# Down projection from 2x2 block products, and a swap of two pools in attention, in a one-core decoder layer

## The chip, the core and the metric

The kernel runs on one core of a Trainium2 chip. The core has five engines with a queue of instructions each: TensorE (PE) multiplies matrices, VectorE (DVE), ScalarE (ACT) and GpSimd (POOL) work on elements, SyncE (SP) mostly issues DMA transfers, which ACT and POOL can issue too. Each engine takes its instructions in the order of its queue, and an instruction whose inputs are not there holds up everything behind it. The metric is the device time of one execution in microseconds (us), lower is better. Three runs of the kernel before gave 1781.09, 1783.0 and 1796.59 us, the median is 1783.0 us.

## The reference

One decoder layer, for a prompt of 1024 tokens and 8 sample tokens (1032 columns in all), in fp32, with D_MODEL = 1024 and D_FF = 2816:

```python
x = x + jnp.concatenate([o_attn, o_gdn], axis=-1) @ w_out   # top-k attention and a gated delta rule
x = x + mem_attend(rmsnorm(x, xattn_norm_g), mem_k, mem_v, w_mq, mq_norm_g, w_mo)
hf = rmsnorm(x, ffn_norm_g)
x = x + (jax.nn.silu(hf @ w_gate) * (hf @ w_up)) @ w_down
```

The change is in the last line's `@ w_down` (2816 rows, 1024 columns) and, by the place of two pools in memory, at the start of `o_attn`.

## The kernel before

Activations lie transposed: features on the 128 partitions, tokens along the free axis. Every fp32 operand is split into a rounded high part and a rest (`wh`, `wl` for weights, `AH`, `AL` for activations, `kh`, `kl` for keys), and every product is three matmuls, high by high, high by rest, rest by high. `split_w` (L125, L126) makes the parts of a weight block with a cast on ACT (`wh`) and a subtraction on POOL (`wl`), each with two buffers; `split` (L143, L144) makes those of an activation with a cast on ACT and a subtraction on DVE.

**Attention.** After the projections, the keys are stacked in `kh` and `kl` (`stack_k`, L490 to L493: ACT casts, POOL copies, a DVE subtraction, in pieces of 256 tokens). The normed queries `qn` are stored to a DRAM scratch `qscr0` to `qscr2` by ACT's queue (L476), and loaded back in blocks of 128 tokens as `qld` by SP's queue (L500) and split into `qst` (L502 to L505, ACT and DVE). The first product of queries and keys is `plg` on PE. `kh` and `kl` lie in the pool `pp`, `qld` and `qst` in `uA`. A pool lies on the left or the right stack of SBUF, and its tiles wait for the last use of whatever lay in the same place: `k1`, the scratch of the top-k searches, was on the right.

**Feed-forward.** The 2816 hidden features are done in 11 units of 256. The gate and up products of a unit already come from 2x2 block products (`unit_product`): sums of weight blocks on DVE (`S`, L1851), their parts on ACT and POOL (`sh`, `sl`, L1856, L1857), and for gate and for up five products of 24 matmuls of 260 columns on PE into `p`, which DVE adds up (`uu`, `s`, L1881); then SiLU on ACT, and three products of gate and up on POOL (L1915), which SP's queue stores to the scratch `scrF`, 22 tiles of 128 features by 1032 tokens. The fourth quarter of each unit (`sg`) is made and stored before the units begin (`early`).

**Down projection.** `stage_down` fetches the tiles back (`fetch`: `af`, then `AH` and `AL` or `dh` and `dl`), in three passes over features 0 to 7, 8 to 14 and 15 to 21. For each of the 8 output blocks of 128 features, `down` loads a weight block (L115, 512 or 448 KB) and multiplies for the token groups of 512, 256 and 264 columns into `pd`: 22 x 8 x 3 x 3 = 1584 matmuls. DVE adds each `pd` into `xT` (L1928), which was loaded with the residual from `scrT` (L1963, L1968). In the last pass `store_y` transposes each finished output block on PE (`py`, L51) and stores it.

The order on each queue is set by a scheduler ahead of time, from its own model of durations and from the order in the program; at run time the queues are fixed.

Of the kernel before, what the change touches and what calls it, by code (L numbers as in the profile page):

```python
# [6 lines left out]
F32 = mybir.dt.float32  # L7
FR = mybir.dt.float32r
BF = mybir.dt.bfloat16
I32 = mybir.dt.int32  # L10
# [3 lines left out]
OP = mybir.AluOpType  # L14
# [25 lines left out]
class Kernel:  # L40
# [111 lines left out]

    def consts(self):
        nc, c = self.nc, self.c
        jp = c.tile([128, 128], I32, name="jp")
# [1660 lines left out]
    def first(self, u, kind, s1, p, sg):  # L1816

        V = self.nc.vector
        if kind == "gate":
            V.tensor_add(sg[:, 0], s1, p)  # L1820
            self.silu(sg[:, 0], sg[:, 0])
        else:
            V.tensor_add(sg[:, 1], s1, p)  # L1823
            self.nc.gpsimd.tensor_mul(sg[:, 1], sg[:, 0], sg[:, 1])
            self.nc.sync.dma_start(self.scrF[2 * u, :, 0:HN], sg[:, 1])

    def unit_product(self, u):

        nc, V = self.nc, self.nc.vector
# [7 lines left out]
        for kind in ("gate", "up"):  # L1837
# [31 lines left out]
            def product(j, op, name):  # L1869
                h, l = parts[j]  # L1870
                banks = []
                for c in halves:
                    p = self.bank("g", name)
                    for k in range(4):
                        self.three(p[:, :w // 2], h[:, k], l[:, k], *ops[op](k, c), k == 0, k == 3)
                    banks.append(p)
                return banks

            def plus(out, x, banks):
                for p, c in zip(banks, halves):  # L1880
                    V.tensor_add(out[:, c], x[:, c], p[:, :w // 2])  # L1881

            if kind == "gate":
# [16 lines left out]
                self.first(u, kind, s1[:, :HN], p, sg[0])  # L1900
            p5 = product(1, "T1", "p5")
            plus(u2, u1, product(3, "T3", "p7"))
            plus(u1, u1, p5)
# [3 lines left out]
            c = [u1, u2[:, :HN], s1]  # L1907
            if kind == "gate":
                for x in c:
                    self.silu(x, x)  # L1910
                sg["c"] = c
            else:
                f = 2 * u
                for x, y, dst in zip(c, sg["c"], (self.scrF[f, :, HN:], self.scrF[f + 1, :, 0:HN], self.scrF[f + 1, :, HN:])):
                    nc.gpsimd.tensor_mul(x, x, y)  # L1915
                    nc.sync.dma_start(dst, x)

    def down(self, f0, acts, groups, last=False):
        nc, V = self.nc, self.nc.vector
        kt = len(acts)  # L1920
        for o in range(KD):
            wh, wl = self.load_w(self.i["w_down"][0][128 * f0:128 * (f0 + kt), 128 * o:128 * o + 128], kt, 128)
            for g in groups:
                g0, n = self.G[g]
                p = self.bank("g", "pd")
                self.proj(wh, wl, 0, 128, g, p, kt=kt, act=lambda k: [x[:, g0:g0 + n] for x in acts[k]])
                x = self.xT[:, o, g0:g0 + n]
                V.tensor_add(x, x, p[:, :n])  # L1928
            if last:
                self.store_y(o)  # L1930

    def store_y(self, o):
        nc = self.nc
        cs = slice(128 * o, 128 * o + 128)
        for half in range(2):
            p = self.bank("g", "py")
            for t in range(4):
                c = 128 * (4 * half + t)
                self.tr(p[:, 128 * t:128 * t + 128], self.xT[:, o, c:c + 128], 128)
            y = self.unit("y", [128, 4, 128])  # L1940
            (nc.vector.tensor_copy if half else nc.scalar.copy)(y, p.rearrange("p (t c) -> p t c", c=128))
            nc.sync.dma_start(self.o["y_prompt"][0, 512 * half:512 * half + 512, cs].rearrange("(t p) c -> p t c", p=128), y)
        p = self.bank("g", "py")
        self.tr(p[:NS, :128], self.xT[:, o, T:NT], 128)
        y = self.unit("y8", [NS, 128])
        nc.scalar.copy(y, p[:NS, :128])
        nc.scalar.dma_start(self.o["y_sample"].rearrange("b o d -> (b o) d")[:, cs], y)

    def fetch(self, f, h, l, s):

        a = self.unit("af")[:, :s.stop - s.start]
        self.nc.sync.dma_start(a, self.scrF[f, :, s])
        self.split(a, h[:, s], l[:, s])

    def stage_down(self, after_units):

        acts = [(self.AH[:, k], self.AL[:, k]) for k in range(KD)]
        n1, n2, n = slice(0, HN), slice(HN, NT), slice(0, NT)
        for f in range(8):
            self.fetch(f, *acts[f], n1)  # L1960
        after_units()
        for o in range(KD):
            self.nc.sync.dma_start(self.xT[:, o, n1], self.scrT[:, o, n1])  # L1963
        for f in range(8):
            self.fetch(f, *acts[f], n2)
        self.down(0, acts, (0,))
        for o in range(KD):
            self.nc.sync.dma_start(self.xT[:, o, n2], self.scrT[:, o, n2])  # L1968
        self.down(0, acts, (1, 2))
        more = [[self.du.tile([128, UW], FR, name="d" + x, tag="d")[:, :NT] for x in "hl"] for _ in range(7)]  # L1970
        for f in range(8, 15):
            self.fetch(f, *more[f - 8], n)
        self.down(8, more, (0, 1, 2))
        for f in range(15, 22):
            self.fetch(f, *acts[f - 15], n)
        self.down(15, acts[:7], (0, 1, 2), True)


    def build(self):
# [7 lines left out]
        self.AH = self.act.tile([128, KD, NT], FR, name="AH")  # L1987
        self.AL = self.act.tile([128, KD, NT], FR, name="AL")
# [30 lines left out]
        for p in (self.sm, self.gp, self.tk, self.hp, self.fp, self.lop, self.wp, self.k1, self.ps):  # L2019
# [18 lines left out]
        for p in (self.pp, self.sm, self.gp, self.late, self.lg, self.up, self.scp, self.keep, self.ps):  # L2038
# [5 lines left out]
        self.scrT, self.scrF = self.dr.tile([128, KD, NT], F32, name="scrT"), self.dr.tile([22, 128, NT], F32, name="scrF")  # L2044
# [16 lines left out]
        self.ps = P(name="psG", bufs=1, space=PSUM)  # L2061
        self.gv = P(name="gv", bufs=1)
        self.gw = P(name="gw", bufs=1)
        for u in range(11):
            self.unit_product(u)

        def after_units():
            for p in (self.tp, self.gw, self.gv):
                p.release()
            self.keep = P(name="keepD", bufs=1)  # L2070
            self.xT = self.keep.tile([128, KD, NT], F32, name="xT")
            self.du = P(name="du", bufs=14)

        self.stage_down(after_units)
        for p in (self.wp, self.du, self.keep, self.u, self.act, self.c, self.dr, self.ps):
            p.release()

    def sample_gen(self):
# [33 lines left out]
```

## Time and profile before

| | |
|---|---|
| runs | 1781.09, 1783.0, 1796.59 us |
| the profiled execution | 1778.02 us, its span 1776.0 us, mean granted PE clock 0.952 |
| busy share | PE 92%, DVE 61%, ACT 50%, POOL 46% |
| the units | from about 1177 to 1500 us |
| the down projection | from about 1500 to 1771 us |

A row of a window gives the busy time of each engine in it and, behind it in brackets, the number of instructions; "PEclk" is the granted clock as a share of full speed, "GB/s" what the DMA engines moved. In a row of the chain of waits stand the start, the time that the piece took and what it was; the chain goes back from the end of the run, so a piece that is not PE is one for which PE stood. A row of an operation gives its name by line, its count, and its shortest, median and longest duration in ns.

### The profile page before, as it was taken

To read this page: it belongs to the slowest core of one execution; us is meant where nothing else is said; L and a number is where in the kernel's file an instruction comes from. 1 tells how busy PE (TensorE), PEld (TensorE's weight loads), DVE (VectorE), ACT (ScalarE), POOL (GpSimd) and SP (SyncE) were. 2 spreads that over 40 slices of the span, in tenths; PEclk is the share of its full clock that TensorE was granted. 3 is DMA by queue.
4 is the path that set the end of the run, shared out by engine and by line. 5 is a ranking of instruction groups with operands and counts; after the bars stand their busy time and mean duration, and the time that the engine had idled before them with its cause. 6 is when DMAs were issued, how large, how long until landed. Compare 5 with 4: busy or idle time off the path is not lost. (4 is left out here: it accounts for less than half of the span.)

```text
span 1776.0 us, 31377 instructions
## 1 busy us (share of the span) xinstructions
PE 1633.0 (92%) x11313; PEld 1439.0 (81%) x11313; DVE 1079.6 (61%) x2767; ACT 881.1 (50%) x2072; POOL 822.8 (46%) x779
## 2 busy tenths in 40 slices
PE   6999988778869999979998899789999999899999
PEld 5998887667747777858887678679999999699998
DVE  7788986999778777752364523775565665313122
ACT  5668879865446666745565564432222322312111
POOL 1277674473274143225453346766666565342210
PEclk9999998879989999979998999989999999899999
DMA  4134343333332233355222335443443444822132
GB/s 157 47 100 132 119 143 125 121 111 111 112 96 72 70 103 101 111 175 151 76 81 63 101 119 184 154 153 118 138 126 117 130 125 149 299 83 86 42 91 58
DMA packets 268628, 206.42 MB, mean 116 GB/s; under 512 B 31397, under 2 KB 240506, under 8 KB 268338
## 3 DMA queue, kind: packets, MB, share of 16 engines
q1 hardware_dynamic: 249674, 175.34, 32.7%
q0 software_dynamic: 4864, 14.69, 2.9%
q10 hardware_dynamic: 13936, 14.40, 2.4%
q8 instruction: 89, 1.46, 0.4%
q14 instruction: 65, 0.53, 0.1%
HBM read 152.01 MB, written 52.47 MB: 115 GB/s over the span
## 5 line engine op out<-in xcount | busy, mean ns | idle before, releaser
L126 POOL TENSOR_TENSOR wl<-raw,wh 128x1024 fp32r<-128x1024 f32 (+2 forms) x107 | 253.8, 2374 | 425.8 <-ACT wh L125 342.1
L48 PE MATMUL pm<-AH,wh 128*128 128x384 f32 (+7 forms) x792 | 267.9, 339 | 3.2 <-ACT wh L125 1.5
L48 PE MATMUL pm<-AH,wl 128*128 128x384 f32 (+7 forms) x792 | 260.9, 330 | 1.0 <-POOL wl L126 1.0
L48 PE MATMUL pm<-AL,wh 128*128 128x384 f32 (+7 forms) x792 | 261.4, 330 | 0.1
L125 ACT CAST wh<-raw 128x1024 fp32r<-128x1024 f32 (+2 forms) x107 | 110.1, 1030 | 267.8 <-PE pd L48 167.5
L48 PEld LDWEIGHTS pm<-AH,wh 128*128 128x128 f32 (+1 forms) x792 | 152.9, 193 | 10.9 <-ACT wh L125 1.9
L1857 POOL TENSOR_TENSOR sl<-S,sh 128x512 fp32r<-128x512 f32 x88 | 119.3, 1366 | 87.3 <-ACT sh L1856 87.3
L48 PEld LDWEIGHTS pm<-AL,wh 128*128 128x128 f32 (+1 forms) x792 | 152.9, 193 | 6.6 <-issue 1.2
L48 PEld LDWEIGHTS pm<-AH,wl 128*128 128x128 f32 (+1 forms) x792 | 152.1, 192 | 5.3 <-POOL wl L126 1.1
L1928 DVE TENSOR_TENSOR xT<-xT,pd 128x256 f32<-128x256 f32 (+2 forms) x72 | 36.7, 511 | 191.9 <-PE pd L48 191.8
L1856 ACT CAST sh<-S 128x512 fp32r<-128x512 f32 x88 | 53.3, 619 | 179.4 <-DVE S L1851 141.5
L48 PE MATMUL pd<-AH,wh 128*128 128x512 f32 (+2 forms) x360 | 117.6, 328 | 5.2 <-ACT wh L125 5.2
L48 PE MATMUL pd<-AH,wl 128*128 128x512 f32 (+2 forms) x360 | 116.8, 326 | 2.4 <-POOL wl L126 2.4
L48 PE MATMUL pd<-AL,wh 128*128 128x512 f32 (+2 forms) x360 | 116.8, 325 | 0.0
L1851 DVE TENSOR_TENSOR S<-raw 128x512 f32<-128x512 f32 x44 | 54.7, 1244 | 95.0 <-DMA raw<-in_w_gate 36.4
L48 PE MATMUL p<-AL,sh 128*128 128x260 f32 x352 | 100.0, 284 | 0.0
L48 PE MATMUL p<-AH,sh 128*128 128x260 f32 x352 | 99.8, 284 | 0.0
L48 PE MATMUL p<-AH,sl 128*128 128x260 f32 x352 | 99.1, 282 | 0.0
L48 PE MATMUL pg<-AH,wh 128*128 128x512 f32 x176 | 74.0, 423 | 13.5 <-DVE sg L1823 7.3
L1881 DVE TENSOR_TENSOR uu<-uu,p 128x260 f32<-128x260 f32 x176 | 71.8, 419 | 16.0 <-PE p L48 14.6
L48 PEld LDWEIGHTS pd<-AH,wh 128*128 128x128 f32 x360 | 69.0, 192 | 12.2 <-ACT wh L125 6.7
L48 PEld LDWEIGHTS pd<-AH,wl 128*128 128x128 f32 x360 | 68.8, 191 | 9.3 <-POOL wl L126 3.8
(702 smaller groups left out, 5108.1 us busy)
## 6 DMA issues: line engine op xcount, KB each, us to landing
raw<-in_w_gate SPq DMA_DIRECT2D x33, 512.0 KB
raw<-in_w_up SPq DMA_DIRECT2D x33, 512.0 KB
raw<-in_w_in SPq DMA_DIRECT2D x24, 512.0 KB
raw<-in_w_out SPq DMA_DIRECT2D x16, 512.0 KB
raw<-in_w_down SPq DMA_DIRECT2D x16, 512.0 KB
af<-scrF SPq DMA_DIRECT2D x14, 516.0 KB
raw<-in_w_down SPq DMA_DIRECT2D x16, 448.0 KB
scrG<-y ACTq DMA_DIRECT2D x32, 192.0 KB
```

Of the source, the lines that this page charges most:

```text
L48: return self.nc.tensor.matmul(out, lhsT, rhs, start=start, stop=stop)
L125: self.nc.scalar.copy(wh, raw)
L126: self.nc.gpsimd.tensor_sub(wl, raw, f32(wh))
L1851: op(t, x, y)
L1856: nc.scalar.copy(h, x)
L1857: nc.gpsimd.tensor_sub(l, x, f32(h))
L1881: V.tensor_add(out[:, c], x[:, c], p[:, :w // 2])
L1928: V.tensor_add(x, x, p[:, :n])
```

## The change

The down projection becomes seven block products. `down_blocks`, a generator that is stepped on in the next unit, makes from a unit's four quarters the seven left factors (activations) and stores them to `scrD[7, 11, 128, 520]`: three POOL products as before, a reload of the early quarter (`bt`), and five DVE operations (L1932 to L1936); in units 0 to 9 the last four stores go by ACT's queue. `stage_down` takes the products in the order A11, A22, S1, S2, S4, S3, A12, each for 4 output blocks with 11 tiles of activations and two blocks of weights (6 and 5 tiles of 128 by 128). The sums of weight blocks are made in place in `Sd` by DVE (L2015 to L2024); the sums of products ("U") are put off until the products have come; the residual is loaded from `scrT` and added later (`residual`); and the activations of a product are fetched during the one ahead of it, into halves of the widened `AH`, `AL` and six tiles `d`. In attention, `uA` (`qld`, `qst`) goes to the right stack, into the place of `k1`, and `pp` (`kh`, `kl`) to the left.

```diff
+                self.last = self.down_blocks(u, (u1, u2, s1), sg["c"])
+                next(self.last)
+    def down_blocks(self, u, up, gate):
+        b12, b21, b22 = up
+        store = lambda j, x, q: q.dma_start(self.scrD[j, u, :, :x.shape[-1]], x)
+        for x, y, j in zip((b12, b22, b21[:, :HN]), (gate[0], gate[2], gate[1][:, :HN]), (0, 5, 6)):
+            G.tensor_mul(x, x, y)
+            if j:
+                store(j, x, nc.sync)
+        yield
...
+        nc.sync.dma_start(b11[:, :HN], self.scrD[0, u, :, :HN])
+        yield
+        V.tensor_sub(t3, b22, b12)
+        V.tensor_sub(b12[:, :HN], b12[:, :HN], b11[:, :HN])
+        V.tensor_sub(t2, b22, b12)
+        V.tensor_sub(t4[:, :HN], b21[:, :HN], t2[:, :HN])
+        V.tensor_scalar(t4[:, HN:], t2[:, HN:], -1.0, None, op0=OP.mult)
+        yield
+        for j, x in ((4, t4), (1, b12), (2, t2), (3, t3)):
+            store(j, x, nc.scalar if u < 10 else nc.sync)
...
+        order = ((0, HN, "A11"), (4, w, "A22"), (1, w, "S1"), (2, w, "S2"), (5, w, "S4"), (3, w, "S3"), (6, HN, "A12"))
...
+        def weights(name, m, ks):
+            t = S[:, m, ks]
+            get = lambda i, j: block(i, j, m, ks, self.wd, 3)
+            if name in ("A11", "A12"):
+                return self.split_w(get(1, int(name[2])) if m and ks.start else block(1, int(name[2]), m, ks, self.wp, 2))
+            if name == "A22":
+                nc.sync.dma_start(t, W[1][:, ks, 512 + 128 * m:512 + 128 * m + 128])
+            elif name == "S1":
+                V.tensor_add(t, t, get(2, 1))
+            elif name == "S2":
+                V.tensor_sub(t, t, get(1, 1))
+            elif name == "S4":
+                V.tensor_sub(t, get(1, 2), t)
+            else:
+                V.tensor_sub(t, get(1, 1), get(2, 1))
+            return self.split_w(t)
...
+            elif name == "S2":
+                add(u)
+                G.tensor_add(c12, c12, u)
+                residual(m + 4, n2)
+            elif name == "S4":
+                add(c12)
+                residual(m, n2)
+                return [(m, 1)]
+            elif name == "S3":
+                add(u)
+                V.tensor_add(c22, c22, u)
+                G.tensor_add(c21, c21, u[:, :HN])
+                return [(m + 4, 1), (m + 4, 0)]
...
+        for q, (_, n, name) in enumerate(order):
+            more = fetches(q + 1, range(11)) if q < 6 else iter(())
+            halves = (slice(0, HN),) if n == HN else (slice(0, w // 2), slice(w // 2, w))
+            for m in range(4):
+                banks = [self.bank("g", "pd") for _ in halves]
+                for ks in (slice(0, 6), slice(6, 11)):
+                    wh, wl = weights(name, m, ks)
+                    for p, c in zip(banks, halves):
+                        for k in range(ks.start, ks.stop):
+                            h, l = slots[q][k]
+                            self.three(p[:, :c.stop - c.start], wh[:, k - ks.start], wl[:, k - ks.start], h[:, c], l[:, c], k == 0, k == 10)
...
-        self.pp = P(name="pp", bufs=1, side="right")
-        self.up = P(name="uA", bufs=1)
+        self.up = P(name="uA", bufs=1, side="right")
         self.lg = P(name="lg", bufs=1)
         self.late = P(name="late", bufs=1)
+        self.pp = P(name="pp", bufs=1)
```

SP's queue at the start of attention, before (`scrV`, `scrX`, `scrY`, `scrA` are the delta rule's scratch, `sst` a state that is loaded for the samples):

```order
L824 DMA scrV_533<-vb_5629 128x512
L834 DMA invY_529<-scrA_536 16x32x32
L1339 DMA sr_ph_6116<-in_page_table 32x8x1 x4
L869 DMA A_6078<-scrA_536 128x2x128
L873 DMA xu_6082<-scrX_537 128x2x32
L873 DMA xu_6082<-scrY_538 128x2x32
L869 DMA A_6097<-scrA_536 128x2x128
L873 DMA xu_6101<-scrX_537 128x2x32
L873 DMA xu_6101<-scrY_538 128x2x32
L1004 DMA sst_6148<-in_state_ssm 128x2x128
L1004 DMA sst_6149<-in_state_ssm 128x2x128
L1004 DMA sst_6150<-in_state_ssm 128x2x128
```

And of the change, at the same place:

```order
L811 DMA scrA_536<-e1_5555 128x4x128
L812 DMA scrQ_534<-e2_5556 128x512
L834 DMA invY_529<-scrA_536 16x32x32
L500 DMA qld_5950<-qscr2_541 128x4x128
L824 DMA scrV_533<-vb_5629 128x512
L500 DMA qld_6609<-qscr2_541 128x4x128
L1339 DMA sr_ph_6116<-in_page_table 32x8x1 x4
L869 DMA A_6078<-scrA_536 128x2x128
```

Before, `qld_5950` stands behind the fourth `sst`; now the first two loads of queries stand ahead of the page table's and the delta rule's loads.

SP's queue where the units end and the down projection begins, before (`uu` and `s1` are quarters of the last units that go to the scratch):

```order
L1952 DMA af_17771<-scrF_10312 128x520
L1916 DMA scrF_10312<-s1_17364 128x520
L1916 DMA scrF_10312<-uu_17544 128x512
L1952 DMA af_18517<-scrF_10312 128x1032
L1952 DMA af_18521<-scrF_10312 128x1032
L1952 DMA af_18525<-scrF_10312 128x1032
L1952 DMA af_18529<-scrF_10312 128x1032
L1916 DMA scrF_10312<-uu_17544 128x520
L1952 DMA af_18533<-scrF_10312 128x1032
L1952 DMA af_18537<-scrF_10312 128x1032
L1952 DMA af_18541<-scrF_10312 128x1032
L1963 DMA xT_17731<-scrT_10311 128x512 x8
```

And of the change (`tt`, `bt` hold the sums of the last unit; `af_17862`, `af_17867` and `af_17872` are the tiles 8, 9 and 10 of A11):

```order
L2009 DMA raw_18093<-in_w_down 128x5x128
L1923 DMA scrD_10312<-uu_17650 128x512
L1963 DMA af_17862<-scrD_10312 128x512
L1963 DMA af_17867<-scrD_10312 128x512
L1923 DMA scrD_10312<-tt_17835 128x520
L1923 DMA scrD_10312<-uu_17650 128x520
L1923 DMA scrD_10312<-bt_17834 128x520
L1963 DMA af_17872<-scrD_10312 128x512
L1923 DMA scrD_10312<-tt_17835 128x520
L1963 DMA af_17902<-scrD_10312 128x520
```

The seven whole tiles and sixteen loads of the residual that stood there are gone; three fetches that the first product needs now stand behind stores of the last unit.

DVE's queue in the down projection, before:

```order
L1928 TENSOR_TENSOR xT_17731<-xT_17731,pd_19001 128x512
L1928 TENSOR_TENSOR xT_17731<-xT_17731,pd_19024 128x256
L1928 TENSOR_TENSOR xT_17731<-xT_17731,pd_19047 128x264
L1928 TENSOR_TENSOR xT_17731<-xT_17731,pd_19076 128x512
L1928 TENSOR_TENSOR xT_17731<-xT_17731,pd_19099 128x256
```

And of the change, in the products A22 and S1 (`raw` is a weight block, `xr` a piece of the residual):

```order
L2020 TENSOR_TENSOR Sd_17857<-Sd_17857,raw_18552 128x640
L144 TENSOR_TENSOR d_18061<-af_18062,d_18061 128x520
L144 TENSOR_TENSOR AL_67<-af_18160,AH_66 128x520
L144 TENSOR_TENSOR AL_67<-af_18164,AH_66 128x520
L2033 TENSOR_TENSOR xT_17855<-xT_17855,pd_18116 128x260
L144 TENSOR_TENSOR AL_67<-af_18203,AH_66 128x520
L2020 TENSOR_TENSOR Sd_17857<-Sd_17857,raw_18603 128x768
L144 TENSOR_TENSOR AL_67<-af_18207,AH_66 128x520
L2033 TENSOR_TENSOR xT_17855<-xT_17855,pd_18117 128x252
L2003 TENSOR_TENSOR xT_17855<-xT_17855,xr_18213 128x512
L2020 TENSOR_TENSOR Sd_17857<-Sd_17857,raw_18654 128x640
```

Where DVE had three additions from PSUM for each output block, it now has splits of activations, weight sums and residuals, all of two inputs from SBUF, among the additions.

## Rows read from the trace of the kernel before

**Rows 1.** The page, its first part: busy us, share of the span, instructions.

```profile
PE 1633.0 (92%) x11313; PEld 1439.0 (81%) x11313; DVE 1079.6 (61%) x2767; ACT 881.1 (50%) x2072; POOL 822.8 (46%) x779
```

**Rows 2.** Windows: length, busy us of PE, PEld, DVE, ACT, POOL, PEclk, DMA share, GB/s.

```profile
1260.00:1270.00 10.00, 10.00 (x86) 10.00 (x85) 7.26 (x15) 3.87 (x7) 7.17 (x6) 1.00 0.23 68
1510.00:1520.00 10.00, 6.72 (x18) 4.56 (x17) 7.68 (x6) 8.51 (x9) 3.83 (x2) 0.66 1.02 382
1520.00:1530.00 10.00, 9.10 (x39) 6.97 (x38) 5.98 (x6) 1.46 (x2) 3.63 (x2) 0.99 1.09 358
1540.00:1550.00 10.00, 6.64 (x18) 4.44 (x17) 0.69 (x1) 2.09 (x2) 4.70 (x2) 0.70 0.47 126
1560.00:1600.00 40.00, 40.00 (x335) 40.00 (x335) 5.96 (x14) 7.21 (x7) 16.57 (x7) 1.00 0.31 90
```

**Rows 3.** The chain of waits from 1234 us on: start, us, what.

```profile
1234.93 242.13 PE p L48 x2016
...
1480.52 4.93 DMA raw<-in_w_down
...
1508.08 7.18 DMA scrF<-uu
...
1534.59 9.55 DMA raw<-in_w_down
...
1545.34 148.68 PE pd L48 x997
1694.02 1.07 PE py L51 x9
1695.09 9.89 PE pd L48 x63
```

**Rows 4.** The timeline of PE at 1507 to 1511 us: start, us, operation.

```profile
1507.64 0.40 PE L48 MATMUL pd<-AH,wh 128*128 128x512 f32 x1
...
1510.66 0.39 PE L48 MATMUL pd<-AL,wh 128*128 128x512 f32 x1
```

**Rows 5.** Operations of single lines, several answers: count, shortest/median/longest ns, first and last.

```profile
L1851 DVE TENSOR_TENSOR S<-raw x44: 691/1462/1798, 1176.2 to 1478.7; 128x512 f32<-128x512 f32 x44
L1851 DVE TENSOR_TENSOR S<-S,raw x22: 682/692/694, 1177.4 to 1474.6; 128x512 f32<-128x512 f32 x22
...
L126 POOL TENSOR_TENSOR wl<-raw,wh x107: 1473/2393/3022, 17.7 to 1749.8; 128x1024 fp32r<-128x1024 f32 x90, 128x896 fp32r<-128x896 f32 x16, 128x608 fp32r<-128x608 f32 x1
...
L125 ACT CAST wh<-raw x107: 681/1047/1117, 16.9 to 1748.8; 128x1024 fp32r<-128x1024 f32 x90, 128x896 fp32r<-128x896 f32 x16, 128x608 fp32r<-128x608 f32 x1
...
L1915 POOL TENSOR_TENSOR s<-s x11: 1300/1312/1325, 1214.3 to 1501.7; 128x520 f32<-128x520 f32 x11
...
L1881 DVE TENSOR_TENSOR uu<-uu,p x176: 408/418/427, 1193.1 to 1504.9; 128x260 f32<-128x260 f32 x176
...
L1856 ACT CAST sh<-S x88: 603/621/628, 1178.2 to 1486.9; 128x512 fp32r<-128x512 f32 x88
```

**Rows 6.** The start of attention, timelines: start, us, operation, idle before and its releaser.

```profile
500.34 1.10 DVE L492 TENSOR_TENSOR kl<-kn,kh 64x256 fp32r<-64x256 f32 x2
...
500.10 2.00 SPq L1004 DMA_DIRECT2D sst<-in_state_ssm  x4
504.88 0.37 SPq L500 DMA_DIRECT2D qld<-qscr  x1
...
508.15 0.62 ACT L502 CAST qst<-qld 64x512 fp32r<-64x512 f32 x1 [8.81 <-DMA kT<-scrG]
...
509.87 0.76 PE L48 MATMUL plg<-kh,qst 128*128 128x512 f32 x1 [13.27 <-DMA vb<-scrV]
```

**Rows 7.** The window of that wait, columns as in Rows 2.

```profile
500.00:510.00 10.00, 0.13 (x1) 0.16 (x1) 6.16 (x17) 1.23 (x2) 9.60 (x19) 0.50 0.65 188
```

**Rows 8.** The start of the output projection, timelines of SP and PE.

```profile
774.75 0.38 SPq L115 DMA_DIRECT2D raw<-in_w_out  x1
...
782.53 0.80 PE L48 MATMUL pm<-AH,wh 128*128 128x512 f32 x1 [1.48 <-ACT wh L125]
```

More of the change, by code (lines that the diff above doesn't have):

```diff
@@ L1918, in down @@
[L1918 to L1930, printed above, removed]
@@ L1933, in store_y @@
+    def store_y(self, o, half):
         nc = self.nc
         cs = slice(128 * o, 128 * o + 128)
-        for half in range(2):
-            p = self.bank("g", "py")
[L1937 to L1942, printed above, removed]
@@ new lines, in store_y @@
+        p = self.bank("g", "py")
+        for t in range(4):
+            c = 128 * (4 * half + t)
+            self.tr(p[:, 128 * t:128 * t + 128], self.xT[:, o, c:c + 128], 128)
+        y = self.unit("y", [128, 4, 128])
+        nc.scalar.copy(y, p.rearrange("p (t c) -> p t c", c=128))
+        nc.scalar.dma_start(self.o["y_prompt"][0, 512 * half:512 * half + 512, cs].rearrange("(t p) c -> p t c", p=128), y)
+        if half:
+            p = self.bank("g", "py")
+            self.tr(p[:NS, :128], self.xT[:, o, T:NT], 128)
+            y = self.unit("y8", [NS, 128])
+            nc.scalar.copy(y, p[:NS, :128])
+            nc.scalar.dma_start(self.o["y_sample"].rearrange("b o d -> (b o) d")[:, cs], y)
@@ new lines, in fetch, with slot, fetches, residual @@
+    def fetch(self, j, u, h, l, early=False):
+        a = self.gw.tile([128, HN], F32, name="af", tag="S", bufs=3) if early else self.unit("af")[:, :h.shape[-1]]
+        self.nc.sync.dma_start(a, self.scrD[j, u, :, :h.shape[-1]])
+        self.split(a, h, l)
+    def stage_down(self, after_units):
+        nc, V, G = self.nc, self.nc.vector, self.nc.gpsimd
+        w = HN + NS
+        order = ((0, HN, "A11"), (4, w, "A22"), (1, w, "S1"), (2, w, "S2"), (5, w, "S4"), (3, w, "S3"), (6, HN, "A12"))
+        W = self.i["w_down"][0].rearrange("(u two p) c -> two p u c", two=2, p=128)
+        n1, n2 = slice(0, HN), slice(HN, NT)
+        def slot(q, u):
+            n = order[q][1]
+            if u < KD:
+                return [t[:, u, w * (q % 2):w * (q % 2) + n] for t in (self.AH, self.AL)]
+            t = self.du.tile([128, 2, w], FR, name="d", tag="d")
+            return [t[:, i, :n] for i in range(2)]
+        def fetches(q, us):
+            for u in us:
+                slots[q].append(slot(q, u))
+                self.fetch(order[q][0], u, *slots[q][u], early=not q and u < KD)
+                yield
+        slots = [[] for _ in order]
+        for _ in fetches(0, range(8)):
+            pass
+        for _ in self.last:
+            pass
+        after_units()
+        for _ in fetches(0, range(8, 11)):
+            pass
+        x, U, S = self.xT, self.U, self.S
+        def residual(o, s, add=True):
+            r = self.unit("xr")[:, :s.stop - s.start] if add else x[:, o, s]
+            nc.sync.dma_start(r, self.scrT[:, o, s])
+            if add:
+                V.tensor_add(x[:, o, s], x[:, o, s], r)
+        G.memset(U[:, :, HN:], 0.0)
+        def block(i, j, m, ks, pool, bufs):
+            t = pool.tile([128, ks.stop - ks.start, 128], F32, name="raw", tag="raw", bufs=bufs)
+            nc.sync.dma_start(t, W[j - 1][:, ks, 512 * (i - 1) + 128 * m:512 * (i - 1) + 128 * m + 128])
+            return t
+        def weights(name, m, ks):
[14 more added lines that the diff above has]
+            return self.split_w(t)
+        def finish(name, m, banks):
+            def add(out):
+                for p, c in zip(banks, halves):
+                    c = slice(c.start, min(c.stop, out.shape[-1]))
+                    V.tensor_add(out[:, c], out[:, c], p[:, :c.stop - c.start])
+            c11, c12, c21, c22 = x[:, m, n1], x[:, m, n2], x[:, m + 4, n1], x[:, m + 4, n2]
+            u = U[:, m]
+            if name == "A11":
+                nc.scalar.copy(u[:, :HN], banks[0])
+                nc.scalar.copy(c11, banks[0])
+            elif name == "S1":
+                for p, c in zip(banks, halves):
+                    nc.scalar.copy(c22[:, c], p[:, :c.stop - c.start])
+                    nc.scalar.copy(c12[:, c], p[:, :c.stop - c.start])
+            elif name == "S2":
[11 more added lines that the diff above has]
+                return [(m + 4, 1), (m + 4, 0)]
+            elif name == "A22":
+                add(c21)
+                residual(m, n1)
+            else:
+                add(c11)
+                return [(m, 0)]
+            return []
+        done = []
+        def store():
+            while done:
+                self.store_y(*done.pop(0))
+        for q, (_, n, name) in enumerate(order):
[5 more added lines that the diff above has]
+                    wh, wl = weights(name, m, ks)
+                    for p, c in zip(banks, halves):
+                        for k in range(ks.start, ks.stop):
+                            h, l = slots[q][k]
+                            self.three(p[:, :c.stop - c.start], wh[:, k - ks.start], wl[:, k - ks.start], h[:, c], l[:, c], k == 0, k == 10)
+                    if q == 1 and not ks.start:
+                        residual(m + 4, n1, False)
+                    for _ in range(2):
+                        next(more, None)
+                    store()
+                done += finish(name, m, banks)
+        store()
```

64 lines of the change are left out of this document (20 added, 44 removed).

## The prediction

> **What bounds it now.** I read the page first: PE is busy 92% of the span, DVE 61%, POOL 46% [rows 1], so the time is PE's work plus the stretches where PE stands. The windows show which is which. Inside the units PE is full at granted clock 1.00 with 86 matmuls of 260 columns in 10 us, and in the later down projection it is full with 335 of 256 and 264 columns in 40 us; where the down projection begins it is not: three windows hold 18, 39 and 18 matmuls while the DMA engines move 382 and 358 GB/s in two of them [rows 2]. The chain of waits says the same: 242 us of nothing but PE in the units, then pieces of weight loads (4.93 us, later 9.55), a store of the last unit (7.18) and, from 1545.34 on, only PE to the end [rows 3]. Two more stretches matter, the start of attention, where PE waited 13.27 us [rows 6], at clock 0.50 in that window [rows 7], and the start of the output projection [rows 8].
>
> **Prices of matmuls.** The chain gives 242.13 / 2016 = 0.120 us for 260 columns [rows 3], the full windows 40 / 335 = 0.119 for 256 and 264 [rows 2], and thirteen steps between the starts of 512-column matmuls take 3.02 us, 0.232 each [rows 4]. A triple of 512, 256 and 264 is then 0.471, and the last blocks agree: 63 matmuls, 21 triples, in 9.89 us [rows 3].
>
> **The down projection, PE.** Before: 528 triples x 0.471 = 249 us. After: two products with 512 columns, 2 x 4 x 11 x 3 = 264 matmuls x 0.232 = 61 us, and five with two halves of 260, 5 x 4 x 11 x 2 x 3 = 1320 x 0.120 = 158; together 220. The change takes **29 us** off PE. At the rate of the window with 86 in 10 us it would be 34, which I keep as an end. The transposes of the output stay.
>
> **Its start.** Before, 146 of the 1584 matmuls were done by 1545.34 (1584 less 997 less 7 x 63 [rows 3]), all of 512 columns: 34 us of work between 1500 and 1545, so about 11.5 us of standing. What stood there, seven whole tiles and sixteen residual loads ahead of the weights, goes. In their place three fetches for A11 stand behind the stores of the last unit. PE has 26 matmuls before it needs tile 8, 6 us; the fetch needs an addition (0.42), a POOL product (1.3), a load of some 5 us, a cast (0.6) and a subtraction (0.7) [rows 3, 5], about 8.5, so PE stands 2.5 us there, and about as much for tile 10, behind four stores. I take 5; ends 0 and 13 (as before). Net **-6.5**.
>
> **New work in the down projection.** A product of two halves has PE for 264 x 0.12 = 31.7 us, 3.96 per weight block on the average, 3.6 for one of five tiles. For it the other engines do the following. ACT: 11 casts and 8 casts of weights, 11 x 0.63 + 8 x 0.73 = 13 us (the weights at 1.047 per 1024 [rows 5]). POOL: 8 subtractions, 5632 columns at 2.39 per 1024 = 13.1 us, and 5.2 more in S2 and S3, four additions of 520 columns like the products of gate and up (1.31). DVE: 11 splits (7.6 at 0.69 each), weight sums over 5632 columns (7.6), residuals (2.8), additions from PSUM (8 x 0.42 = 3.4) [rows 5]: 21 us. Each is hidden behind 31.7 us of PE, if each ran alone. But an operation of two SBUF inputs on DVE took 0.69 us in all 22 cases of one form and up to 1.80, median 1.46, in the other form of the same size [rows 5], which runs beside POOL. So I add DVE's SBUF work and POOL's as if only one could run: A22 7.6 + 2.8 + 13.1 = 24; S1 with the residual of A22 31; S2 7.6 + 7.6 + 2.8 + 18.3 = 36; S4 31; S3 36. S1 to S3 make 134 us beside 127 of PE, so about 7 are not covered. The weights' way to PE in one block is a sum (1.05), a cast (0.78) and a subtraction (1.8), 3.6 us with nothing in between, against 3.6 to 4.3 of PE with two buffers; a late member shows at once, and ACT's casts of activations stand in the same queue. I add 5 to 6 us for that: **+13** in all. Lower end 0, all covered; the upper end is the rival below.
>
> The row alone shows the long duration and not why. The Trainium skill, SBUF — State Buffer, "Who interferes with whom", says that a DVE instruction with two SBUF inputs shares a read interface with GpSimd's reads, and that the later one blocks for the whole instruction. By that rule the sum of the two engines' times is the right count, and an addition from PSUM (one SBUF input) is free of it; the trace agrees, 408 to 427 ns in 176 cases [rows 5]. If they ran freely side by side, the term would be 5 to 6 and not 13.
>
> **The units.** Each gets five DVE operations of 520 columns, one of a single input: 3.5 us, up to 9 beside POOL, on an engine busy 7.3 of 10 us [rows 2], and four more DMA transfers. 28.8 us of PE cover them (240 matmuls x 0.120); without slack each unit would lose up to 9 - 0.27 x 28.8 = 1 us. I take 0, ends 0 and +10.
>
> **Attention's start.** PE's wait ended with the first `plg`; ahead of it were the casts of `qst` at 508.15, its load issued at 504.88 behind the loads of `sst`, which SP issued until 502.10, while the last `kl` was ready at 501.44 [rows 6]. After, the queries' loads stand ahead and `qst` can be ready before the keys. Then `plg` starts near 502, **-8**. Ends 0 (the keys come later in their turn, as DVE also has 6.2 us of other work in that window [rows 7]) and -13.
>
> **Output projection.** The first weights, issued at 774.75, were what PE waited for at 782.53 [rows 8]. In the changed order three stores of the samples' state, two loads of the samples' input and a second `xn` stand ahead of that load on SP, where single issues take about 0.4 us (0.38 there): **+2**, ends 0 and +5, if some of them wait.
>
> **Sum.** -29 - 6.5 + 13 - 8 + 2 = -28.5 on the profiled 1778.0: 1749.5. The median of the runs shown lies 5 us above that execution and the lowest 3, so the forecast is a little higher, **1751**.
>
> **Rivals.**
> *Everything covered.* DVE and POOL take turns without loss; PE stands nowhere new. For it: DVE has 0.3 to 0.4 of a unit free today, and the units run full beside POOL. 1751 - 13 = 1738, some 1735 with the upper rate of PE. Chance 0.14.
> *Late transfers.* The activations now come as 77 fetches of up to 260 KB, the weights as 64 blocks, some 43 MB in 230 us, 190 GB/s, beside 382 in the crowd [rows 2]. For it: loads of 512 KB took 4.9 us alone and up to 9.6 in the crowd [rows 3]; weight blocks are three ahead, 12 us. Against it: half the load that made the crowd. If each of the six changes of product costs 4 us: +24, 1775. Chance 0.18.
> *The weights' chain sets the pace* (the other side). In S1, S2, S4 and S3 a weight sum of 704 columns takes up to 2.5 us beside POOL (1.80 per 512), the cast (0.72) may stand behind one of an activation (0.63), and the subtraction takes 1.65: 5.5 us a block in place of 3.96, on 32 blocks +49, and with the granted clock that such standing brought in the crowd (0.66 and 0.70 [rows 2]) some 10 more: 1751 - 13 + 59 = 1797. It decides from a block period of 5.3 us on, where 32 x 1.35 = 43 eats the four gains. For it: the sums wait on DMA, ACT, DVE and POOL in turn. Against it: the units have the same chain in blocks of 512 columns and run full. By the rule of the Trainium skill named above (SBUF — State Buffer, "Who interferes with whom") the two engines' turns, 36 us for the 8 blocks of S2 or S3, would make 4.5 us a block, short of that point. Chance 0.08, half of it beyond 1801.
> *Attention does not gain.* The swap moves the wait from queries to keys: 1759. Chance 0.06.
> The forecast has the remaining 0.54, its own range 1738 to 1766.
>
> **Range and chances.** 1725 to 1785 leaves out most of the third rival and a tenth beyond the ends of the terms. A change under 1% (18 us) can't be told from none here. Faster than 1765: nearly all of the forecast, the first and fourth rival, and a third of the second, **0.75**; within 1%: 0.18; slower: 0.07, half of the third rival and the far ends of late transfers and of the units.
>
> **What would show it.** The stretch from the last `p` to the last `pd` near 241 us without transposes and not 271; windows of S1 and S2 with 77 or more matmuls in 10 us; DVE's weight sums over 1.4 us per 768 columns where POOL works; PE's wait ahead of the first `plg` 5 us and not 13; units still at 28.8 us each. I am wrong where PE in the units stands, where its waits in S1 to S3 are for `wh` at every block, or where attention ends as late as before.

## The result, and the profile after

The changed kernel has a median of 1793.03 us in seven runs (1785.66 to 1800.06), the kernel before 1781.5 (1774.25 to 1796.59): a ratio of 1.0062, with a 95% interval of 1.0039 to 1.0085. It is slower by 0.6% where I forecast 1751, and outside the range of 1725 to 1785. The profiled execution is the fastest of the seven; its span of 1783.9 us is 7.9 more than before, while the medians are 11.5 apart. Where the 7.9 come from is read from the starts of the first and last matmul of each tile:

| stretch of the profiled executions | before | after | difference |
|---|---|---|---|
| start to the first matmul into `p` | 1178.9 | 1172.6 | -6.3 |
| units: first to last `p` | 320.9 | 351.7 | +30.8 |
| down projection: last `p` to last `pd` | 270.7 | 253.6 | -17.1 |
| last `pd` to the end | 5.5 | 6.0 | +0.5 |

The page, its first part, beside [rows 1]:

```profile
PE 1607.8 (90%) x11313; PEld 1420.5 (80%) x11313; DVE 1178.9 (66%) x2873; ACT 928.7 (52%) x2175; POOL 872.2 (49%) x812
```

PE has 25 us less to do and the run is longer: PE stands where it did not. Windows of the changed kernel, columns as in [rows 2], show it in the units, as the prediction's last paragraph named for a sign of being wrong:

```profile
1340.00:1350.00 10.00, 8.52 (x71) 8.34 (x70) 8.80 (x15) 1.86 (x3) 7.46 (x6) 1.00 0.65 196
1350.00:1360.00 10.00, 10.00 (x84) 9.82 (x82) 5.11 (x10) 3.05 (x5) 3.35 (x3) 1.00 0.37 123
```

Where [rows 2] had 86 matmuls in 10 us, one of these windows has 71, with DVE at 8.8 of 10. The chain of waits, which in [rows 3] was one piece of PE of 242 us, now goes round the same way in the third to the tenth unit. One turn of it:

```profile
1338.09 1.26 POOL uu L1925
...
1339.74 1.30 POOL sl L1857
...
1341.06 0.06 DVE S L1851
...
1343.18 1.38 DVE tt L1932
...
1344.81 1.45 DVE uu L1933
...
1346.29 0.71 DVE bt L1934
...
1347.02 0.69 DVE tt L1935
1347.71 0.08 DVE tt L1936
1347.79 0.34 DVE uu L1881
1348.13 0.02 ACTq L1923
...
1348.25 0.63 ACT sh L1856
...
1348.91 0.64 POOL sl L1857
...
1349.57 5.00 DMA raw<-in_w_gate
...
1354.65 0.70 DVE S L1851
...
1357.40 0.84 POOL sl L1857
...
1358.26 1.76 DVE S L1851
1360.02 0.35 DVE uu L1881
...
1360.50 10.33 PE p L48 x84
```

The new sums (L1932 to L1936) stand between the sums `S` of one pair of weight blocks and the cast and subtraction that give the second block's buffer back. They meet on ACT's queue, at `ACTq L1923`: there the stores of the sums stand ahead of that cast, and the cast waits with them. The same cast in a unit of the kernel before, where it waited for PE, and then in the turn above (the number in brackets is the idle time of ACT before it, and what ended it):

```profile
1361.86 0.62 ACT L1856 CAST sh<-raw 128x512 fp32r<-128x512 f32 x1 [1.00 <-PE p L48]
```

```profile
1347.49 0.62 ACT L1856 CAST sh<-raw 128x512 fp32r<-128x512 f32 x1 [3.94 <-DVE bt L1934]
```

The next load of gate weights is issued the moment that buffer is free, takes 5 us, and DVE waits for it with the additions that free PSUM banks, where PE's products go, behind it. From the product on POOL at 1338.09 to the matmul at 1360.50 the turn takes 22.4 us; PE starts 168 matmuls in that time, 20.2 us of work. SP's queue, the kernel before and then the changed one, shows the late load:

```profile
1332.53 0.38 SPq L1841 DMA_DIRECT2D raw<-in_w_gate  x1
1333.00 1.70 SPq L1916 DMA_DIRECT2D scrF<-uu  x1
1336.19 0.38 SPq L1841 DMA_DIRECT2D raw<-in_w_gate  x1
```

```profile
1342.87 0.38 SPq L1841 DMA_DIRECT2D raw<-in_w_gate  x1
1343.34 0.53 SPq L1930 DMA_DIRECT2D bt<-scrD  x1
1347.01 0.32 SPq L1887 DMA_DIRECT2D s<-scrS  x1
1349.57 0.38 SPq L1841 DMA_DIRECT2D raw<-in_w_gate  x1
```

The second gate load follows the first after 3.7 us before and after 6.7 now, the same to a tenth in 7 of 11 units. That is 3.0 us, and the units grew by 30.8 / 10 = 3.1 each on the average, but the agreement is no proof: unit by unit the growth is 6.0 in the third, 2.1 to 2.4 in the next four and 3.0 to 4.1 in the last four, and before the change one pair stood 7.4 us apart while PE did not wait. What has PE waiting, from the first unit's start to the last unit (total, times, longest):

```profile
PE p L48 <- DVE uu L1881: 19.8, 22, 1.6
PE p L48 <- ACT sh L1856: 2.9, 2, 1.6
```

The name is that of the last link, an addition on DVE. In the turn above PE stands twice for one:

```profile
1348.27 0.36 PE L48 MATMUL p<-T2h,sh 128*128 128x260 f32 x1 [1.48 <-DVE uu L1881]
1360.50 0.36 PE L48 MATMUL p<-AH,sh 128*128 128x260 f32 x1 [0.47 <-DVE uu L1881]
```

The first addition stands right behind the sums on DVE's queue (1347.79 in the chain); the second comes after the late load. Nine of the waits, 1.3 to 1.6 us each and 13.0 us together, are of the first kind, straight behind the sums (two of them name the cast behind the stores); the others come after waits of DVE for loads or for POOL, or in the last unit. So the sums cost in two places, ahead of the additions and ahead of the cast.

### The profile page after: what moved, and what is told of

Its sections match the earlier page's. It is cut to its first block, busy times and chain, and to the rows that moved or that the text cites. A ratio compares the mean times of both kernels' runs of the same rounds, so it can differ in the third digit from the quotient of the medians.

```text
span 1783.9 us, 31956 instructions
## 1 busy us (share of the span) xinstructions
PE 1607.8 (90%) x11313; PEld 1420.5 (80%) x11313; DVE 1178.9 (66%) x2873; ACT 928.7 (52%) x2175; POOL 872.2 (49%) x812
## 5 line engine op out<-in xcount | busy, mean ns | idle before, releaser
L126 POOL TENSOR_TENSOR wl<-raw,wh 128x1024 fp32r<-128x1024 f32 (+2 forms) x91 | 208.5, 2294 | 228.1 <-ACT wh L125 228.0
L1857 POOL TENSOR_TENSOR sl<-S,sh 128x512 fp32r<-128x512 f32 x88 | 123.0, 1408 | 89.1 <-ACT sh L1856 82.9
L125 ACT CAST wh<-raw 128x1024 fp32r<-128x1024 f32 (+2 forms) x91 | 90.6, 997 | 113.1 <-PE pm L48 35.0
L48 PE MATMUL pd<-AH,wl 128*128 128x260 f32 (+1 forms) x384 | 114.5, 307 | 5.8 <-POOL wl L126 5.8
L126 POOL TENSOR_TENSOR wl<-Sd,wh 128x768 fp32r<-128x768 f32 (+1 forms) x40 | 77.0, 1928 | 87.2 <-ACT wh L125 85.8
L48 PE MATMUL pd<-AH,wh 128*128 128x260 f32 (+1 forms) x384 | 115.4, 304 | 2.1 <-ACT wh L125 2.1
L48 PE MATMUL pd<-AL,wh 128*128 128x260 f32 (+1 forms) x384 | 114.7, 303 | 0.0
L48 PEld LDWEIGHTS pd<-AH,wh 128*128 128x128 f32 x384 | 72.7, 189 | 5.8 <-ACT wh L125 3.1
L144 DVE TENSOR_TENSOR AL<-af,AH 128x520 fp32r<-128x520 f32 (+1 forms) x56 | 52.2, 954 | 34.8 <-ACT AH L143 34.5
```

The source lines that it names most:

```text
L48: return self.nc.tensor.matmul(out, lhsT, rhs, start=start, stop=stop)
L125: self.nc.scalar.copy(wh, raw)
L126: self.nc.gpsimd.tensor_sub(wl, raw, f32(wh))
L144: self.nc.vector.tensor_sub(l, src, f32(h))
L1857: nc.gpsimd.tensor_sub(l, x, f32(h))
```

## The experiments

Each was timed beside the kernel before on the same chip. "Units" is first to last `p` in its profile, "pair" the time between the two loads of a unit's gate weights, and of its up weights, as most of the units have it.

| run | units | pair, gate / up | ratio to before, interval |
|---|---|---|---|
| before | 320.9 | 3.7 / 3.3 | |
| changed | 351.7 | 6.7 / 3.3 | 1.0062 (1.0039 to 1.0085) |
| stores on SP | 353.4 | 7.3 / 3.3 | 1.0078 (1.0052 to 1.0104) |
| no sums | 323.1 | 3.7 / 3.3 | 0.9891 (0.9851 to 0.9932) |
| swap alone | 321.3 | 3.7 / 3.3 | 1.0008 (0.998 to 1.0036) |
| sums later | 346.9 | 3.7 / 5.9 | 1.0043 (1.0015 to 1.0072) |
| sums in the gap | 340.3 | 3.3 / 4.9 | 1.0026 (1.001 to 1.0043) |
| the same, stores on ACT | 342.1 | 3.3 / 4.9 | one time, 1785.96 us |
| sums on POOL | 333.8 | 6.2 / 3.3 | 0.9945 (0.9921 to 0.9968) |
| loop loosened | 328.0 | 3.7 / 2.4 | 0.9921 (0.989 to 0.9952) |
| loosened, on POOL | 339.2 | 3.7 / 1.2 to 1.6 | 0.9992 (0.9968 to 1.0016) |
| before, loosened | 328.8 | 3.7 / 2.0 | 1.0002 (0.9978 to 1.0025) |
| loosened, no swap | 329.2 | 3.7 / 2.4 | 0.9899 (0.987 to 0.9928) |
| all together | 351.3 | 2.4 / 2.4 | 1.0054 (1.0036 to 1.0071) |

The pair alone does not set the units: with all edits together the gate pair is the shortest and the units are as long as in the changed kernel, with the sums on POOL it is nearly as long as there and the units are 18 us shorter.

**Stores by SP's queue.**

```diff
-            store(j, x, nc.scalar if u < 10 else nc.sync)
+            store(j, x, nc.sync)
```

> Edit: the four stores of the sums of a unit go by SP's queue in all units, not by ACT's in units 0 to 9. Three theories of why the units (first to last matmul into p) took 351 us and not 320. ACT's queue: casts stand behind stores that wait for DVE's sums, so a raw weight buffer comes free late and the next gate load starts late; then the units fall to 330 or less and the run to about 1765. DVE's work: the five sums themselves, and their wait for POOL's products, hold up the additions that free PSUM banks, and the stores are bystanders; then the units stay at 345 to 351 and the run at 1780 to 1786. DMA load: six stores and a reload per unit slow the weight loads; then no change, 351 and 1784.

Units 353.4, run 1.0078: taking the stores off ACT's queue brings nothing. The cast no longer waits, but on SP's queue the stores stand ahead of the second gate load itself, which comes 7.3 us after the first: one waiting instruction for another. So this run does not show that a store ahead of a waiting cast is free, only that the place of the stores is not the whole cause.

**No sums.** The five DVE lines and the reload out, `(4, b21), (1, b12), (2, b22), (3, b22)` stored.

> Edit: leaves out the five sums of a unit on DVE and the reload of its early quarter; the quarters themselves are stored in their place, by the same queues, with the same bytes stored. ACT's queue: the stores now wait for POOL's products alone, some 3 us less, and the units fall to about 330, not all the way. DVE's work: the units go back to 320 to 323 and the run to about 1753. DMA load: the stored bytes are the same and the reload is a seventh of the added traffic, so the units stay near 347 and the run near 1780.

Units 323.1, run 0.9891. The sums, and with them the reload, make 28.6 of the 30.8 us; the stored bytes make the other 2.2 at most. Load on the DMA engines falls as the main cause.

**The swap alone.**

```diff
-        self.pp = P(name="pp", bufs=1, side="right")
-        self.up = P(name="uA", bufs=1)
+        self.up = P(name="uA", bufs=1, side="right")
...
+        self.pp = P(name="pp", bufs=1)
```

> Edit: the kernel before with the swap of the two pools of attention alone. If the 6.7 us by which the units began earlier in the changed kernel come from the swap, the run is 6 to 7 us below the kernel before, some 1770 profiled, with the first product of queries and keys near 494 us; if they come from the other edits (the small constant moved to another pool), it is the same as before.

Ratio 1.0008. The first `plg` came at 504.2, 5.7 us earlier than in [rows 6] but not at 494, and the first `p` at 1185.0, 6 later. In the three profiles without the swap (the kernel before, its loosened version, and the last but one run below) the first `p` comes at 1178.9, 1186.9 and 1169.6, in the eleven with it at 1172.6 to 1186.3: one profile to the next differs there by 17 us, far more than the 6.3 I had read as the swap's gain.

**The sums later.**

```diff
+        self.behind(V.tensor_sub(t3, b22, b12), self.gate_end)
...
+            self.behind(store(j, x, nc.sync), self.raw_up)
```

(`behind` orders an instruction after others on its queue; the load of `s1` stands behind `raw_up` too.)

> Edit: the sums of a unit are ordered behind the last addition of the next unit's gate part on DVE, its four stores go by SP's queue behind the next unit's second up load or later, and the load of the next s1 stands behind that load too, not ahead of the second gate load. ACT's queue: no cast waits for sums, units at 325 or less, run about 1757. DVE's work: the same 5.5 us of sums per unit on DVE, so if only their amount matters the units stay at 340 or more; if their place matters (no wait for POOL's products there, no load behind them) the units fall to 325 too. DMA load: the same transfers, units near 351, run 1784.

Units 346.9. The delay moved with the sums: the gate pair is back at 3.7 and the up pair, 3.3 before, is at 5.9. Amount on DVE and place in the loop both fit, so the next runs part them.

**The sums in the gap**, all stores on SP, and a twin with the stores on ACT.

```diff
+        self.behind(V.tensor_sub(t3, b22, b12), self.add)    # behind the p5 additions
...
+                self.behind(op(t, x, y), self.sums)          # S behind the sums
```

> Edit: the five sums of a unit are ordered on DVE behind the p5 additions of the next unit's gate part and ahead of the next sums S of weights, that is into the stretch where DVE stood 4 to 4.5 us for a weight load and POOL is idle; the stores go by SP's queue. Two theories are left of why the units take 31 us more. Place: the sums stand between the additions that free PSUM banks, on top of the backlog that DVE has after its wait for weights, and beside POOL's subtractions, so they cost 1.0 to 1.8 us each; in the gap they cost 0.7, nothing waits behind them, and the units fall to 325 or less, the run to 1765 or less (median). Amount: DVE has no room for five more operations wherever they stand; the units stay at 343 to 351, the run at 1785 to 1793.

The first sum in the changed kernel, in this run, and in the run with the loosened loop (count, shortest/median/longest ns):

```profile
L1932 DVE TENSOR_TENSOR tt<-s,uu x11: 1437/1452/2291, 1213.4 to 1530.3; 128x520 f32<-128x520 f32 x11
```

```profile
L1941 DVE TENSOR_TENSOR tt<-s,uu x11: 692/693/694, 1215.2 to 1521.3; 128x520 f32<-128x520 f32 x11
```

```profile
L1933 DVE TENSOR_TENSOR tt<-s,uu x11: 701/1769/1782, 1217.6 to 1509.1; 128x520 f32<-128x520 f32 x11
```

Here the first sum took 0.69 us in every unit, and the units still took 340.3. But the order has a cost of its own: PE now waited for casts (`ACT sh`, 15.9 us), since `S` stands behind the sums. So this run does not say how much of the 31 us came from the longer operations. My 325 was a miss. The twin,

> Edit: as in the run with the sums in the gap, but the four stores stay on ACT's queue in units 0 to 9. If stores on ACT's queue cost anything by themselves, the units are longer than there by over 3 us; if they are bystanders, as the run with all stores on SP's queue says, within 3 us of it.

had 342.1 and one time, 1785.96: with the sums early on DVE, the stores are bystanders on either queue.

**The sums on POOL.** `V.tensor_sub` became `G.tensor_sub` in four lines.

> Edit: four of the five sums of a unit are done by POOL and not by DVE (the fifth, of 8 columns, stays). Place and amount on DVE: DVE's queue holds no more SBUF work than before the change, so the units fall to 330 or less, unless POOL, at 1.3 us for each (5.2 us more per unit beside 17 of 29), delays its subtractions and so the weights. Room of the two engines together (work on two SBUF inputs and POOL's count as one engine): POOL's longer operations make it worse, units 355 or more, run 1798 or more.

Units 333.8, run 0.9945. That theory of one common room for DVE and POOL, on which this run should have been the worst, falls.

**The loop loosened.**

```diff
-                t = self.gw.tile([128, 4, 128], F32, name="S", tag="S", bufs=3)
+                t = self.gw.tile([128, 4, 128], F32, name="S", tag="S", bufs=4)
...
-                h, l = (self.gw.tile([128, 4, 128], FR, name="s" + y, tag="s" + y, bufs=7) for y in "hl")
+                h, l = (self.gw.tile([128, 4, 128], FR, name="s" + y, tag="s" + y, bufs=7 if y == "h" else 6) for y in "hl")
...
+            t3 = total(a11, a21)
             halve(2, t2)
+            halve(5, a22)
             halve(1, t1)
-            halve(3, total(a11, a21))
-            halve(5, a22)
+            halve(3, t3)
```

> Edit: the changed kernel with the weights' loop of the units loosened: a fourth buffer for the sums S of weights (one buffer of the rests sl less), and the quarter that comes straight from the loaded block cast and subtracted second and not fourth, so that both raw buffers come free some 4 to 5 us sooner; the sums of activations stay where they are, on DVE, and the stores on ACT's queue. Theory of the weights' loop: a half unit has 14.4 us of PE, and the way from a raw buffer's release over the load (5 us), S, casts and subtractions to its next release takes nearly as long, so that any work put into that way lengthens the unit; then loosening it brings the units to 330 or less and the run to 1770 or less. Theory of DVE's room: DVE's additions are late because DVE and POOL together have too much; then the units stay at 343 to 351 and the run at 1785 to 1793.

Units 328.0, run 0.9921: faster than both kernels, with the sums still on DVE, in their old place, and longer than ever (1769 ns, above). DVE was busy 222 of 300 us here, 203 with the stores on SP, where the units took 353. So DVE was not out of room there. The edit does two things, and no run parts them: the fourth buffer lets DVE make `S` earlier (its waits for POOL there fall from 23.5 us to 5.2), and the cast that frees the second block now stands ahead of the stores on ACT's queue. What PE still waits for after the first unit, 0.2 to 2.3 us in seven units, is again the addition right behind the sums. SP's queue in this run has the pair at 3.65 us again, although the reload still stands inside it:

```profile
1332.48 0.37 SPq L1841 DMA_DIRECT2D raw<-in_w_gate  x1
1332.94 1.53 SPq L1924 DMA_DIRECT2D scrD<-uu  x1
1334.56 0.38 SPq L1931 DMA_DIRECT2D bt<-scrD  x1
1336.13 0.38 SPq L1841 DMA_DIRECT2D raw<-in_w_gate  x1
```

**Loosened, with the sums on POOL.**

> Edit: the loosened loop, and four of the five sums on POOL. Loop: both edits take work out of the same loop, so units at 320 to 325 and the run near 1758 to 1764, below the kernel before by 1% and more. DVE's room: no further gain beyond the run with the sums on POOL, units 334, run 1771.

A miss: the two edits do not add up. Units 339.2; the loads come in time (pairs of 3.7 and 1.2 to 1.6), and PE waited for additions of DVE (`s`, 11.3 us). POOL was busy 229 of 300 us; what in it held DVE up was not followed further.

**The kernel before, loosened.**

> Edit: the kernel before with the loop loosened in the same way and nothing else. Both theories: PE is full in its units already, so the units stay at 320 to 322 and the run within 0.3% of the kernel before. If it is faster by more, the gain of the loosened kernels is not the loop's slack taken back but something the kernel before had lost too.

Ratio 1.0002, as expected, though its profile shows 328.8 in the units, not 320 to 322, and a down projection 6 us shorter. The kernel before gains nothing from the edit, so what it gives the changed kernel is what the change had lost there. The two 328 are not the same loss: here PE was full in the second to sixth unit and stood in the seventh to tenth, after waits of DVE for loads and behind splits for the down projection that came early, not behind sums.

**Loosened, without the swap.**

> Edit: the kernel with the loosened loop, but with the two pools of attention where the kernel before has them. It was 0.9921 of the kernel before with the swap. If the swap brings the 6 us that the first product of the units was earlier by in the changed kernel's profile, this run is about 0.9955 and the first product of queries and keys near 510 us; if what it gains at the start of attention is given back by the end of that stage, as the run with the swap alone says (1.0008), it stays within 0.002 of 0.9921.

0.9899 (0.987 to 0.9928), median 1763.09 beside 1781.88: the best version that computes the whole layer. With the swap it was 0.9921, the intervals overlap; the swap brings nothing that these runs can see. Here the first `plg` came at 500.4, without the swap and not at 510, so the other edits move it too.

**All together.** Loosened loop, sums in the gap, transposes one weight block later.

> Edit: the changed kernel with the loosened loop, the sums of a unit in DVE's gap behind the p5 additions of the gate part, and in the down projection the transposes of a finished block one weight block later, behind the residual's addition. Loop: with the sums off the way to the bank-freeing additions too, units at 321 to 325 (328 with the loop alone) and 5 us less standing before transposes: the run near 1758, 0.987 of the kernel before. If the sums in the gap delay S again and with it the casts, as in the run without the loosened loop (340), units stay at 328 or more and the run at 0.990 to 0.993.

1.0054, units 351.3: a miss. PE waited for casts 23 times (20.0 us), which waited for `S` (80.5 us on ACT). The fixed order that puts `S` of the next half unit behind the sums takes away the lead that the loosened loop had given. The later transposes were no gain either: 6.3 us of waits for the residual's addition before, as after.

## Why the prediction was wrong

**The step that failed** is "The units": "28.8 us of PE cover them ... I take 0, ends 0 and +10". It measured +30.8, three times the end of its range. The work was within what was counted, 3.5 to 9 us: four sums of 0.7 to 1.45 us and one on 8 columns (and not on 520), 4.4 us a unit by the medians. It was weighed against the wrong thing, DVE's busy share of 7.3 in 10. DVE's idle time was not room: it is waiting in a chain that no busy share shows, buffer free, load of 5 us, `S`, cast, subtraction, buffer free, twice in a unit, with the additions for PE in the same queue. That PE was full said only that this chain was no longer than PE's 28.8, not how much shorter. The waits of DVE in the kernel before, from 1200 to 1500 us:

```profile
DVE S L1851 <- DMA raw<-in_w_gate: 36.4, 10, 5.4
DVE S L1851 <- DMA raw<-in_w_up: 29.9, 9, 4.8
...
DVE uu L1881 <- PE p L48: 17.6, 21, 3.3
```

The waits for loads do not tell how much room there was. In the loosened kernel before, at 1.0002 of the same time, they are longer (and also in the second to sixth unit, where PE was full in both: 49 us and 41):

```profile
DVE S L1851 <- DMA raw<-in_w_up: 44.8, 10, 5.9
DVE S L1851 <- DMA raw<-in_w_gate: 42.5, 8, 8.5
```

The last row of the first view says more: only there did DVE wait for PE and not for its own chain, 17.6 us in some ten units, 1.7 a unit. In the changed kernel no such wait is left. An estimate from it, made after the result, is 4.4 of sums less 1.7 of lead, 2.7 us a unit, against 3.1 measured; no run tests it. How the 30.8 us divide between the sums ahead of the additions and the sums ahead of the cast stays open.

**The third rival** had the nearest mechanism, the weights' way through DVE, ACT and POOL, in the wrong stage. What I held against it, that "the units have the same chain ... and run full", was the place where a chain of that kind cost.

**The down projection** was right in kind and a quarter short: -17.1 where -29 - 6.5 + 13 makes -22.5. PE's work is as priced; from the changed kernel's chain, 260 columns take 7.69 / 64 = 0.120 us and 512 take 7.64 / 33 = 0.232:

```profile
1724.29 7.69 PE pd L48 x64
...
1759.17 7.64 PE pd L48 x33
```

220 and 8.6 for the transposes (eight times the 1.07 of [rows 3]) leave 25 us of standing, against 18 forecast, 5 at the start and 13 for the new work. The waits name 20 of them, and the largest row was in no term:

```profile
PE py L51 <- DVE xT L2003: 6.1, 3, 3.5
PE pd L48 <- POOL wl L126: 5.8, 8, 1.9
PE pd L48 <- ACT d L143: 4.7, 1, 4.7
PE pd L48 <- ACT wh L125: 2.1, 2, 1.5
```

The transposes wait for the residual that is now added late (6.1). The wait at the start was 4.7 (5 forecast), the weights' chain 7.9 beside 13. The 13 had two parts, and the larger, 7 us because DVE's sums and POOL take turns, did not show as forecast: the sums of S1 took 0.81 to 0.95 us, where the prediction named over 1.4 as its sign.

```profile
L2020 DVE TENSOR_TENSOR Sd<-Sd,raw x8: 810/886/947, 1562.8 to 1592.8; 128x768 f32<-128x768 f32 x4, 128x640 f32<-128x640 f32 x4
```

In the window with the most traffic of this stage, 289 GB/s, PE was busy for 47.5 of 50 us:

```profile
1550.00:1600.00 50.00, 47.52 (x338) 44.32 (x337) 33.65 (x41) 24.18 (x38) 22.77 (x12) 1.00 0.99 289
```

No wait of PE in this stage names a load, and those for the weights' chain are far from the 59 us of the third rival: neither of the two rivals came.

**Attention's start** moved as said and further, the first `plg` at 494.20 and not 502:

```profile
494.20 1.19 PE L48 MATMUL plg<-kh,qst 128*128 128x512 f32 x2 [4.53 <-POOL kl L493]
499.34 0.79 PE L48 MATMUL plg<-kh,qst 128*128 128x512 f32 x1 [3.52 <-DVE ast L527]
```

But what starts 6 to 16 us earlier ends no earlier on the average: swap alone 1.0008. In the profile after, PE then waits for DVE's maxima (`ast`), and the stretch from the first `plg` to the first `p` is 678 us and not 669. That the units began 6.3 us earlier, where -8 + 2 was forecast, is luck, by the spread of 17 us above. The fourth rival has the outcome, and the wait did move to the keys in part (4.53 us). What paces the rest of that stage stays open; it wasn't followed.

**Output projection:** +2 forecast. The first weights were issued 10.2 us after the first `xn` load and not 1.9, and the first `pm` came at 781.46, 1.1 us earlier than in [rows 8] in a stage that began 7 earlier: 6 us, above the end of 5.

**DVE and POOL.** The Trainium skill, SBUF — State Buffer, "Who interferes with whom", was cited for the down projection; the units are where it shows, 1452 ns for a sum beside POOL and 693 for the same sum away from it. That lengthening alone does not make the 31 us: with the loop loosened the sum took 1769 ns and the units 328.0.

## What to carry to other kernels

Before work is put beside a full engine, find the chain that feeds it: from a load buffer's release round to its next release, through every engine, with every queue in which an instruction that waits can hold up a step of it. Busy shares do not tell its room, and waits for its loads do not either: here they were 66 us before, 87 in the same kernel loosened, and 24 in a run whose units took 351 us. How long an engine waits for the full one was a better sign here (17.6 us before, none after), as long as what the full engine needs from elsewhere comes in time. Work of 4.4 us a unit in front of the steps that free buffers and banks cost 3.1 us a unit here. Then release buffers earlier first (here a quarter cast sooner, one more small buffer: 0.9921 in place of 1.0062), and add the work after.

## What the runs showed of the hardware that was not expected

An operation on 8 columns, the last of the sums, took 0.16 us in the changed kernel (median of 11) and 1.26 us in the run with the loosened loop, where POOL was at work beside it:

```profile
L1936 DVE TENSOR_SCALAR tt<-bt x11: 162/164/1258, 1218.7 to 1534.7; 128x8 f32<-128x8 f32 x11
```

```profile
L1937 DVE TENSOR_SCALAR tt<-bt x11: 156/1259/1267, 1222.5 to 1513.4; 128x8 f32<-128x8 f32 x11
```

It has a single SBUF input. The Trainium skill, SBUF — State Buffer, "Who interferes with whom", counts such an operation among those that can wait for GpSimd in a faster mode with two ports; no run here shows in which mode it ran.
